# Forgetting bias in the scores' accumulation: one table of cumulative sums for block 1's attention

## The chip, the cores and the metric

The kernel runs on one core of a Trainium2 chip. The metric is the device time of one execution in microseconds (us). The engines are PE (TensorE, matmuls; PEld is its weight load), DVE (VectorE), ACT (ScalarE), POOL and SP; SP issues the weight transfers. Lines of the kernel are written L1204.

## What is computed

Two transformer blocks run one after the other on 256 tokens of width 1024. Block 1 has a causal pooling branch and a "forgetting" attention of 16 heads of 64, block 2 has two other attentions, and each block ends with a retrieval layer over 16384 experts. Only the forgetting attention is touched by the change:

```python
F = jnp.transpose(jnp.cumsum(log_f.astype(jnp.float32), axis=1), (0, 2, 1))
...
    s = jnp.einsum('bqhd,bkhd->bhqk', q[:, q0:L], k[:, :L]) * scale
    s = s + F[:, :, q0:L, None] - F[:, :, None, :L]
    s = jnp.where(kpos[None, :] <= qpos[:, None], s, NEG_INF)
    p = jax.nn.softmax(s, axis=-1).astype(v.dtype)
```

`log_f` is one number for each token and head. A score gets the cumulative sum at its query's position and loses the one at its key's. The first of the two is the same along a row of scores, and a softmax over the row does not depend on it.

## The kernel before

Both blocks are written as one program in which each engine's order is the order of the code. A `Stream` loads the weights in units of 1 MB through SP into three raw buffers (`raw`), ACT makes the high half (`hi`, L138) and DVE the low half (`lo`, L141), and PE multiplies in three passes (hi by hi, lo by hi, hi by lo). In the mixer of block 1 the function `mm_et` (L442) makes a quarter of q, k, the pooling input or the gates from two half units of 24 matmuls each, and `mm_te` (L484) makes v. The units' order is `names1`: v0 q0 k0 v1 q1 k1 p0 p1 v2 q2 k2 v3 q3 k3 a0 to a3 b0 to b3. Results go to two PSUM tiles (`mm`) in turn, and ACT takes them out: kT and qT at L1320, the gates `sga` at L1330 with a sigmoid, for which ACT loads another table than for the exponentials.

Attention is woven in between these groups of 24. `Weave.tick` is called after each group and runs at most four tasks. One of them is `attn_all`, which keeps up to four pairs of heads alive and at each tick moves at most two of them one step on; `attn(hp)` is a generator whose `yield`s are the ends of its steps. There are eight pairs. A pair's steps before the change are:

1. The bias: PE makes for each head of the pair the sum of `lf` up to each key, spread over all 128 rows, by multiplying with the constant `ncum` (-8 on and above the diagonal; 8 is what the scale of the scores takes back): L1204 adds up the first 128 tokens for all 256 keys, L1206 the second 128 tokens for the keys 128 to 255. DVE adds the query's own sum `f8` and the causal mask to it and writes `fm` (L1210, 256 columns, and L1212, 128 columns).
2. The scores: PE multiplies q and k, 64 rows for a head, the first head of the pair on rows 0 to 63 and the second on rows 64 to 127 (L1222 with 256 columns for the second query block, L1223 with 128 for the first). DVE adds `fm` and takes the maximum (L1226, L1228), and ACT makes the exponentials (L1232, L1234).
3. DVE multiplies with the reciprocal of the sums.
4. PE transposes the weights (L1246 to L1248), DVE and ACT copy them to `pt`.
5. PE multiplies with v (L1258, L1260), 64 result rows for a head, and ACT copies the result to `oT`.

All of the attention's operands are fp32, and each of its matmuls is executed as two instructions; the weight matmuls are one instruction each. `forget` makes `lf` ahead of all this from the forget logits (L1176, L1183), and at its end `f8` with three small matmuls (L1194 to L1196).

Of the kernel before, what the change touches and what calls it, by code (L numbers as in the profile page):

```python
# [9 lines left out]
F32 = mybir.dt.float32  # L10
# [4 lines left out]
OP = mybir.AluOpType  # L15
AX = mybir.AxisListType

S = 256
# [4 lines left out]
LOWEST = -3.0e38  # L23
# [11 lines left out]
WHOLE = (18,)  # L35
Y1, Y2, Y3, Y4 = 1, 2, 3, 3
WIDE1 = 1
# [159 lines left out]
def kernel(  # L197
# [29 lines left out]
    V, A, PE, GP = nc.vector, nc.scalar, nc.tensor, nc.gpsimd  # L227
# [9 lines left out]

    # ---------------------------------------------------------- constants
    xpool = [ctx.enter_context(ExitStack())]
# [19 lines left out]
    ident = keep.tile([128, 128], F32, name="ident")  # L259
# [11 lines left out]

    # ---------------------------------------------------------- modulation
    modc = [keep.tile([128, 6, 8], F32, name=f"modc{b}") for b in range(2)]
# [83 lines left out]
    order = [(b, j) for b in range(2) for j in (1, 0, 2, 3, 4, 5)]  # L357
# [9 lines left out]

    # ---------------------------------------------------------- unit order
    last_v, first_v, xnext = [], [], []
# [55 lines left out]

    # ---------------------------------------------------------- helpers
    small = ctx.enter_context(tc.tile_pool(name="small", bufs=2))
# [184 lines left out]

    # ---------------------------------------------------------- PEER
    def peer(b, plan, keys_d, gelu, xs):
# [472 lines left out]

    # ---------------------------------------------------------- block 1 mixer
    with ExitStack() as mx:
        pa = mx.enter_context(tc.tile_pool(name="mix1", bufs=1))  # L1090
# [3 lines left out]
        cs = {k: ct[:, a - 128:b - 128] for k, (a, b) in off.items() if a >= 128}  # L1094
# [5 lines left out]
        def at():  # L1100
            return ps.tile([128, 512], F32, name="at", tag="at")
# [7 lines left out]
        qT = pa.tile([128, 8, S], F32, name="qT")  # L1109
        kT = pa.tile([128, 8, S], F32, name="kT")  # L1110
# [12 lines left out]
        r = rsqrt_seed([ms[:, tt:tt + 1] for tt in range(2)], base)  # L1123
# [42 lines left out]
        lf = pa.tile([128, 2, 16], F32, name="lf")  # L1166
        f8 = pa.tile([128, 2, 16], F32, name="f8")

        def forget():
            split_small(wf, wfh, wfl)  # L1170
            yield 1
            p = at()
# [8 lines left out]
            p = at()  # L1181
# [11 lines left out]
            p = at()  # L1193
            PE.matmul(p[:, 0:16], lhsT=cs["ncum"][:, 0:128], rhs=lf[:, 0, :], start=True, stop=True)  # L1194
            PE.matmul(p[:, 16:32], lhsT=cs["ncum"][:, 128:256], rhs=lf[:, 0, :], start=True, stop=False)
            PE.matmul(p[:, 16:32], lhsT=cs["ncum"][:, 0:128], rhs=lf[:, 1, :], start=False, stop=True)  # L1196
            V.tensor_scalar(f8.rearrange("p a b -> p (a b)"), p[:, 0:32], -1.0, None, op0=OP.mult)

        def attn(hp):
            fm = pa.tile([128, 2, 384], F32, name="fm", tag="fm", bufs=1)  # L1200
            p = at().rearrange("p (a k) -> p a k", a=2)
            for j in range(2):
                h = 2 * hp + j
                PE.matmul(p[:, j, :], lhsT=lf[:, 0, h:h + 1].to_broadcast([128, 128]),  # L1204
                          rhs=cs["ncum"], start=True, stop=False)
                PE.matmul(p[:, j, 128:256], lhsT=lf[:, 1, h:h + 1].to_broadcast([128, 128]),  # L1206
                          rhs=cs["ncum"][:, 0:128], start=False, stop=True)
            for j in range(2):
                h = 2 * hp + j
                V.scalar_tensor_tensor(fm[:, j, 0:256], p[:, j, :], f8[:, 1, h:h + 1],  # L1210
                                       cs["cmask"], op0=OP.add, op1=OP.add)
                V.scalar_tensor_tensor(fm[:, j, 256:384], p[:, j, 0:128], f8[:, 0, h:h + 1],  # L1212
                                       cs["cmask"][:, 128:256], op0=OP.add, op1=OP.add)
            yield Y1
            pm = pa.tile([128, 2, 384], F32, name="pm", tag="pm", bufs=LIVE)
# [3 lines left out]
            for j in range(2):  # L1219
                r = slice(64 * j, 64 * j + 64)  # L1220
                p = at()
                PE.matmul(p[:, 0:256], lhsT=qT[r, hp, 128:256], rhs=kT[r, hp, :], start=True, stop=True)  # L1222
                PE.matmul(p[:, 256:384], lhsT=qT[r, hp, 0:128], rhs=kT[r, hp, 0:128], start=True, stop=True)  # L1223
                tiles.append(p)
            for j in range(2):
                V.tensor_tensor_reduce(pm[:, j, 0:256], tiles[j][:, 0:256], fm[:, j, 0:256], 1.0, LOWEST,  # L1226
                                       OP.add, OP.max, m[:, 2 * j:2 * j + 1])
                V.tensor_tensor_reduce(pm[:, j, 256:384], tiles[j][:, 256:384], fm[:, j, 256:384], 1.0, LOWEST,  # L1228
                                       OP.add, OP.max, m[:, 2 * j + 1:2 * j + 2])
            V.tensor_scalar(m, m, -0.125, None, op0=OP.mult)  # L1230
# [117 lines left out]

    # ---------------------------------------------------------- block 2 mixer
    with ExitStack() as mx:  # L1350
# [310 lines left out]
```

## Time and profile before

| | |
|---|---|
| median of 3 runs | 2098.63 us |
| lowest and highest run | 2094.62, 2100.15 us |
| span of the profiled execution | 2093.1 us |
| median of the runs less that span | 5.5 us |
| PE busy | 2050.3 us (98%) |
| DVE busy | 1603.1 us (77%) |
| ACT busy | 986.8 us (47%) |

The profiled execution has no time of its own beside its span; the span runs from its first to its last instruction. "Busy" counts a matmul from its start to its modelled end, and these overlap, so how long a matmul holds PE is read from the starts of the ones that follow each other. In the rows a matmul's shape in the array stands as rows*columns: 128*128 is the whole array, 64*128 half of its rows, 128*64 half of its columns, 16*128 sixteen rows.

### The profile page before, as it was taken

How to read it: one execution, taken by the hardware profiler on the slowest of the kernel's cores; microseconds unless marked ns; L12 is line 12 of the kernel's file. 1: busy time of each engine (PE TensorE's matmuls, PEld its weight loads, DVE VectorE, ACT ScalarE, POOL GpSimd, SP SyncE). 2: the span in 40 equal slices, each digit the busy share in tenths (PEclk: the TensorE clock that was granted, in tenths of full speed). 3: DMA queues.
4: the chain of work that ended last, by engine and by line, in shares of the span. 5: the costliest groups of instructions: out<-in, count | busy, mean ns of one | idle time of the engine just before them, and what ended most of it. 6: DMA issues, size and time to landing. Idle time of an engine off the chain costs nothing.

```text
span 2093.1 us, 37810 instructions
## 1 busy us (share of the span) xinstructions
PE 2050.3 (98%) x15694; PEld 1885.9 (90%) x15694; DVE 1603.1 (77%) x2937; ACT 986.8 (47%) x1307; POOL 5.6 (0%) x15
## 2 busy tenths in 40 slices
PE   5999999999999999999999999999999999999998
PEld 4999999999999877888899999999999998778886
DVE  6787698868876799777668557988588766996556
ACT  4446455544344434444554455555443444344444
POOL 0000000000000000000000000000000000000000
PEclk8999999999999999999989999999999999999999
DMA  8555545554447644588445345555544475445563
GB/s 346 210 218 202 181 164 198 183 184 171 165 168 266 239 161 163 208 333 306 184 174 201 132 141 182 180 183 184 199 163 162 165 259 200 156 168 181 190 222 121
DMA packets 57211, 408.83 MB, mean 195 GB/s; under 512 B 6352, under 2 KB 6736, under 8 KB 8016
## 3 DMA queue, kind: packets, MB, share of 16 engines
q1 hardware_dynamic: 55424, 397.76, 53.4%
q0 software_dynamic: 1296, 8.52, 1.2%
q8 instruction: 123, 2.02, 0.4%
q14 instruction: 48, 0.39, 0.1%
q10 hardware_dynamic: 320, 0.14, 0.0%
HBM read 403.26 MB, written 3.15 MB: 194 GB/s over the span
## 4 chain that ended last, share of the span: by engine, by line
PE 91%; DVE 4%; ACT 2%; DMA 2%; issue 1%; SPq 0%; ACTq 0%; DVEq 0%
PE mm L442 46%; PE acc L897 31%; PE mm L484 2%; PE mm L580 2%; PE g L834 2%; PE g L835 1%; DVE lo L141 1%; PE acc L984 1%; DVE macc L334 1%; DMA raw<-in_w_in_dram 1%; ACT hi L138 1%; PE g L766 1%; PE acc L880 1%; PE mm L458 1%; PE mm L290 0%
## 5 line engine op out<-in xcount | busy, mean ns | idle before, releaser
L141 DVE TENSOR_TENSOR lo<-raw,hi 128x1024 fp32r<-128x1024 f32 x632 | 766.2, 1221 | 366.2 <-ACT hi L138 365.0
L138 ACT ACTIVATE hi<-raw 128x1024 fp32r<-128x1024 f32 x632 | 663.5, 1055 | 490.8 <-PE acc L897 226.5
L442 PE MATMUL mm<-hhi,hi 128*128 128x256 f32 x2848 | 399.8, 282 | 1.9 <-ACT sga L1330 1.6
L442 PE MATMUL mm<-hlo,hi 128*128 128x256 f32 x2848 | 392.9, 280 | 0.0
L442 PE MATMUL mm<-hhi,lo 128*128 128x256 f32 x2848 | 392.7, 280 | 0.0
L442 PEld LDWEIGHTS mm<-hhi,hi 128*128 128x128 f32 x2848 | 359.8, 188 | 6.2 <-ACT sga L1330 1.8
L442 PEld LDWEIGHTS mm<-hhi,lo 128*128 128x128 f32 x2848 | 358.0, 188 | 0.0
L442 PEld LDWEIGHTS mm<-hlo,hi 128*128 128x128 f32 x2848 | 357.9, 188 | 0.0
L897 PE MATMUL acc<-hi,whi 128*128 128x512 f32 x976 | 307.1, 396 | 0.7 <-ACT whi L545 0.7
L897 PE MATMUL acc<-lo,whi 128*128 128x512 f32 x976 | 301.9, 391 | 0.0
L897 PE MATMUL acc<-hi,wlo 128*128 128x512 f32 x976 | 300.6, 389 | 0.0
L897 PEld LDWEIGHTS acc<-hi,wlo 128*128 128x128 f32 x976 | 183.2, 188 | 39.6
L897 PEld LDWEIGHTS acc<-lo,whi 128*128 128x128 f32 x976 | 183.2, 188 | 39.1
L897 PEld LDWEIGHTS acc<-hi,whi 128*128 128x128 f32 x976 | 177.2, 188 | 33.5 <-ACT whi L545 1.6
L636 ACT ACTIVATE ringa<-mm 128x512 f32<-128x512 f32 x80 | 47.9, 599 | 111.6 <-PE mm L442 111.6
L827 DVE TENSOR_TENSOR gg<-b,gT 128x512 f16<-128x512 f16 x256 | 96.2, 417 | 0.0
L824 DVE TENSOR_TENSOR b<-iota,idx2T 128x1024 f16<-128x1024 f16 x128 | 87.5, 683 | 0.0
L545 ACT ACTIVATE whi<-ringa 128x512 fp32r<-128x512 f32 x78 | 48.8, 628 | 77.3 <-PE acc L897 77.3
L834 PEld LDWEIGHTS <-b 128*128 128x128 f16 x1024 | 63.4, 98 | 20.2 <-issue 8.3
L834 PE MATMUL g<-gg,b 128*128 128x64 f16 x1024 | 78.2, 194 | 0.1
L835 PE MATMUL g<-gg,b 128*128 128x64 f16 x1024 | 77.0, 193 | 0.0
L636 ACT ACTIVATE ringb<-mm 128x512 f32<-128x512 f32 x48 | 28.7, 599 | 93.8 <-PE mm L442 93.8
(359 smaller groups left out, 1837.5 us busy)
## 6 DMA issues: line engine op xcount, KB each, us to landing
raw<-in_peer_u_dram SPq DMA_DIRECT2D x128, 1024.0 KB, 4.9
raw<-in_peer_v_dram SPq DMA_DIRECT2D x118, 1024.0 KB, 4.9
raw<-in_w_in_dram SPq DMA_DIRECT2D x45, 1024.0 KB, 5.0
raw<-in_w_mod_dram SPq DMA_DIRECT2D x20, 1024.0 KB, 5.0
raw<-in_w_ada_dram SPq DMA_DIRECT2D x20, 1024.0 KB, 5.4
ringa<-in_peer_v_dram SPq DMA_DIRECT2D x10, 1024.0 KB, 5.6
raw<-in_w_out_dram SPq DMA_DIRECT2D x8, 1024.0 KB, 4.9
raw<-in_w_query_dram SPq DMA_DIRECT2D x8, 1024.0 KB, 4.9
```

The source lines that it names most:

```text
L138: self.nc.scalar.activation(hi, src, AF.Copy)
L141: self.nc.vector.tensor_sub(lo, src, hi.bitcast(F32))
L442: PE.matmul(ps[:, j, :], lhsT=w[:, k, :], rhs=h[:, k, :], start=n == 0 and k == 0, stop=n == 2 and k == 7)
L484: PE.matmul(ps[:, tt, :], lhsT=h[:, 4 * p + k, tt * 128:(tt + 1) * 128], rhs=w[:, k, :], start=p == 0 and tt == 0 and i == 0, stop=p == 1 ...
L545: A.activation(hi, src, AF.Copy)
L580: PE.matmul(acc[q][:, tt, :], lhsT=h[:, 4 * p + k, tt * 128:(tt + 1) * 128], rhs=w[:, k, :], start=p == 0 and tt == 0 and i == 0, stop=p = ...
L636: state["evac"] = lambda: A.activation(slots(p), ps, gelu)
L824: V.tensor_tensor(pairs(b2), lanes(0, 128), each(idx2T[:, c], 128), op=OP.is_equal)
L827: V.tensor_tensor(pairs(gg[:, :, i, :]), pairs(b1), each(gT[:, c, i, :], 64), op=OP.mult)
L834: PE.matmul(ps[:, t, :], lhsT=b2[:, t, :], rhs=gg[:, t, 0, :], start=True, stop=False)
L835: PE.matmul(ps[:, t, :], lhsT=b2[:, t, :], rhs=gg[:, t, 1, :], start=False, stop=True)
L897: PE.matmul(acc[tt][dh], lhsT=w[:, j, tt * 128:(tt + 1) * 128], rhs=v[:, dh * 512:(dh + 1) * 512], start=p == 0 and j == 0 and n == 0, sto ...
```

## The change

`forget` ends with another table: `fk`, 16 rows (one for each head) by 256 tokens, with -8 times the cumulative sum. Two matmuls make it (256 and 128 columns, 16 result rows), and DVE copies it to SBUF. `attn` has no step for the bias any more: for each head a matmul with a column of the identity, spread to 128 columns, picks the head's row of `fk` and writes it on all 128 rows of the scores' PSUM tile, and the matmul of q and k adds to it. DVE adds the constant mask in place of `fm`. `fm`, `f8` and their DVE passes are gone, and with them the query's own sum.

```diff
-        f8 = pa.tile([128, 2, 16], F32, name="f8")
+        fk = pa.tile([16, S], F32, name="fk")
...
-            PE.matmul(p[:, 0:16], lhsT=cs["ncum"][:, 0:128], rhs=lf[:, 0, :], start=True, stop=True)
-            PE.matmul(p[:, 16:32], lhsT=cs["ncum"][:, 128:256], rhs=lf[:, 0, :], start=True, stop=False)
-            PE.matmul(p[:, 16:32], lhsT=cs["ncum"][:, 0:128], rhs=lf[:, 1, :], start=False, stop=True)
-            V.tensor_scalar(f8.rearrange("p a b -> p (a b)"), p[:, 0:32], -1.0, None, op0=OP.mult)
+            PE.matmul(p[0:16, 0:256], lhsT=lf[:, 0, :], rhs=cs["ncum"], start=True, stop=False)
+            PE.matmul(p[0:16, 128:256], lhsT=lf[:, 1, :], rhs=cs["ncum"][:, 0:128], start=False, stop=True)
+            V.tensor_copy(fk, p[0:16, 0:256])
 
         def attn(hp):
-            fm = pa.tile([128, 2, 384], F32, name="fm", tag="fm", bufs=1)
-            p = at().rearrange("p (a k) -> p a k", a=2)
-            for j in range(2):
-                h = 2 * hp + j
-                PE.matmul(p[:, j, :], lhsT=lf[:, 0, h:h + 1].to_broadcast([128, 128]),
-                          rhs=cs["ncum"], start=True, stop=False)
-                PE.matmul(p[:, j, 128:256], lhsT=lf[:, 1, h:h + 1].to_broadcast([128, 128]),
-                          rhs=cs["ncum"][:, 0:128], start=False, stop=True)
-            for j in range(2):
-                h = 2 * hp + j
-                V.scalar_tensor_tensor(fm[:, j, 0:256], p[:, j, :], f8[:, 1, h:h + 1],
-                                       cs["cmask"], op0=OP.add, op1=OP.add)
-                V.scalar_tensor_tensor(fm[:, j, 256:384], p[:, j, 0:128], f8[:, 0, h:h + 1],
-                                       cs["cmask"][:, 128:256], op0=OP.add, op1=OP.add)
-            yield Y1
...
             for j in range(2):
                 r = slice(64 * j, 64 * j + 64)
                 p = at()
-                PE.matmul(p[:, 0:256], lhsT=qT[r, hp, 128:256], rhs=kT[r, hp, :], start=True, stop=True)
-                PE.matmul(p[:, 256:384], lhsT=qT[r, hp, 0:128], rhs=kT[r, hp, 0:128], start=True, stop=True)
+                row = ident[0:16, 2 * hp + j:2 * hp + j + 1].to_broadcast([16, 128])
+                PE.matmul(p[:, 0:256], lhsT=row, rhs=fk, start=True, stop=False)
+                PE.matmul(p[:, 0:256], lhsT=qT[r, hp, 128:256], rhs=kT[r, hp, :], start=False, stop=True)
+                PE.matmul(p[:, 256:384], lhsT=row, rhs=fk[:, 0:128], start=True, stop=False)
+                PE.matmul(p[:, 256:384], lhsT=qT[r, hp, 0:128], rhs=kT[r, hp, 0:128], start=False, stop=True)
                 tiles.append(p)
             for j in range(2):
-                V.tensor_tensor_reduce(pm[:, j, 0:256], tiles[j][:, 0:256], fm[:, j, 0:256], 1.0, LOWEST,
+                V.tensor_tensor_reduce(pm[:, j, 0:256], tiles[j][:, 0:256], cs["cmask"], 1.0, LOWEST,
                                        OP.add, OP.max, m[:, 2 * j:2 * j + 1])
```

The line numbers move: in the changed kernel the bias matmuls are L1207 and L1209, the scores L1208 and L1210, the maximum L1213 and L1215, the exponentials L1219 and L1221, the product with v L1245 and L1247, the gate's evacuation L1317.

PE's order at the first pair of heads, where the first four matmuls of the bias stood before and all eight of the pair stand now:

```order
-L1204 MATMUL at<-cst_108,lf 128x256
-L1206 MATMUL at<-cst_108,lf 128x128
-L1204 MATMUL at<-cst_108,lf 128x256
-L1206 MATMUL at<-cst_108,lf 128x128
+L1207 MATMUL at<-fk,ident 128x256
+L1208 MATMUL at<-kT,qT 128x256
+L1209 MATMUL at<-fk,ident 128x128
+L1210 MATMUL at<-kT,qT 128x128
+L1207 MATMUL at<-fk,ident 128x256
+L1208 MATMUL at<-kT,qT 128x256
+L1209 MATMUL at<-fk,ident 128x128
+L1210 MATMUL at<-kT,qT 128x128
```

The scores stood a group of 24 weight matmuls later, four in a row; now they stand a step earlier and take turns with the bias, and the second head's bias comes between the two heads' scores.

PE's order before at the last pair of heads, whose scores (L1222, L1223) stand right behind another pair's product with v (L1258, L1260); L1300 is a product of the pooling branch:

```order
252 L1258 MATMUL at<-pt,vv 64x256
253 L1260 MATMUL at<-pt,vv 64x128
254 L1258 MATMUL at<-pt,vv 64x256
255 L1260 MATMUL at<-pt,vv 64x128
256 L1222 MATMUL at<-kT,qT 128x256
257 L1223 MATMUL at<-kT,qT 128x128
258 L1222 MATMUL at<-kT,qT 128x256
259 L1223 MATMUL at<-kT,qT 128x128
260 L1300 MATMUL at<-pl,wp 128x256 x2
```

PE's order now at the last pair of heads, from its second head on:

```order
237 L1207 MATMUL at<-fk,ident 128x256
238 L1208 MATMUL at<-kT,qT 128x256
239 L1209 MATMUL at<-fk,ident 128x128
240 L1210 MATMUL at<-kT,qT 128x128
241 L442 MATMUL mm<-hhi,hi 128x256 x8
242 L442 MATMUL mm<-hhi,lo 128x256 x8
243 L442 MATMUL mm<-hlo,hi 128x256 x8
244 L1245 MATMUL at<-pt,vv 64x256
```

A pair's scores now end before a group of weight matmuls and have the product with v behind that group; at three of the eight pairs they followed directly on such a product before, and now at none.

ACT's order around the first gate before (L1330), where the last pair's exponentials (L1232, L1234) come behind two gates:

```order
94 L1330 ACT_TABLE_LOAD
95 L1330 ACTIVATE sga<-mm 128x512
96 L138 ACTIVATE hi<-raw 128x1024 x2
97 L1262 ACTIVATE oT<-at 128x256
98 L1330 ACTIVATE sga<-mm 128x512
99 L138 ACTIVATE hi<-raw 128x1024
100 L1262 ACTIVATE oT<-at 128x256
101 L1232 ACT_TABLE_LOAD
102 L1232 ACTIVATE pm,al<-pm,am 128x256
103 L1234 ACTIVATE pm,al<-pm,am 128x128
```

and now, where the last pair's exponentials (L1219, L1221) stand ahead of the first gate (L1317):

```order
94 L138 ACTIVATE hi<-raw 128x1024
95 L1219 ACTIVATE pm,al<-pm,am 128x256
96 L1221 ACTIVATE pm,al<-pm,am 128x128
97 L1219 ACTIVATE pm,al<-pm,am 128x256
98 L1221 ACTIVATE pm,al<-pm,am 128x128
99 L1317 ACT_TABLE_LOAD
100 L1317 ACTIVATE sga<-mm 128x512
101 L138 ACTIVATE hi<-raw 128x1024
102 L1249 ACTIVATE oT<-at 128x256
```

The last pair moved from behind the gates to ahead of them, and one table load to the exponentials' table and one back are gone.

## Rows read from the trace of the kernel before

**Rows 1.** The page's first part: busy time, share, instructions of each engine.

```profile
span 2093.1 us, 37810 instructions
PE 2050.3 (98%) x15694; PEld 1885.9 (90%) x15694; DVE 1603.1 (77%) x2937; ACT 986.8 (47%) x1307; POOL 5.6 (0%) x15
```

**Rows 2.** Busy time in stretches of 20 us; columns in the first line.

```profile
core 0: us, PE busy (x) PEld busy (x) DVE busy (x) ACT busy (x) POOL busy (x), PEclk, DMA share, GB/s
...
20.00:40.00 20.00, 11.24 (x61) 11.07 (x62) 18.60 (x31) 8.63 (x16) 0.00 (x0) 0.57 0.77 297
...
140.00:160.00 20.00, 19.72 (x160) 18.58 (x158) 15.13 (x33) 9.08 (x18) 0.00 (x0) 1.00 0.54 195
160.00:180.00 20.00, 18.72 (x152) 17.90 (x153) 16.34 (x38) 14.89 (x25) 0.00 (x0) 1.00 0.61 213
...
220.00:240.00 20.00, 18.02 (x132) 17.73 (x131) 14.88 (x38) 10.51 (x25) 0.00 (x0) 0.83 0.30 106
```

**Rows 3.** What PE waited for, 40 to 240 us: total, times, longest.

```profile
PE mm L442 <- ACT sga L1330: 1.6, 1, 1.6
PE at L516 <- DVE modc L300: 1.2, 1, 1.2
```

**Rows 4.** Groups by line, 56 to 176 us: busy us, mean ns, idle before.

```profile
L1210 DVE SCALAR_TENSOR_TENSOR fm<-at,f,cst 128x256 f32<-128x256 f32 x16 | 7.6, 475 | 1.3 <-PE at L1206 1.3
...
L1212 DVE SCALAR_TENSOR_TENSOR fm<-at,f,cst 128x128 f32<-128x128 f32 x16 | 5.5, 341 | 0.0
```

**Rows 5.** PE's timeline at the first pair: start, us, instructions merged.

```profile
63.66 0.64 PE L484 MATMUL mm<-lo,hhi 128*128 128x256 f32 x4
64.14 0.63 PE L484 MATMUL mm<-hi,hlo 128*128 128x256 f32 x4
64.69 0.71 PE L1222 MATMUL at<-kT,qT 64*128 64x256 f32 x4
65.23 0.40 PE L1223 MATMUL at<-kT,qT 64*128 64x128 f32 x4
65.55 0.70 PE L1204 MATMUL at<-cst,lf 128*128 128x256 f32 x2
66.09 0.38 PE L1206 MATMUL at<-cst,lf 128*128 128x128 f32 x2
66.31 0.60 PE L1204 MATMUL at<-cst,lf 128*128 128x256 f32 x2
66.74 0.38 PE L1206 MATMUL at<-cst,lf 128*128 128x128 f32 x2
66.88 1.18 PE L442 MATMUL mm<-hhi,hi 128*128 128x256 f32 x8
```

**Rows 6.** PE's timeline at the last pair, scores behind a product with v.

```profile
164.27 0.66 PE L1258 MATMUL at<-pt,vv 128*64 128x256 f32 x4
164.76 0.40 PE L1260 MATMUL at<-pt,vv 128*64 128x128 f32 x4
165.08 0.71 PE L1222 MATMUL at<-kT,qT 64*128 64x256 f32 x4
165.62 0.40 PE L1223 MATMUL at<-kT,qT 64*128 64x128 f32 x4
```

**Rows 7.** PE's timeline in `forget`: the 16-row transposes, and f8's matmuls.

```profile
47.17 1.09 PE L442 MATMUL mm<-hlo,hi 128*128 128x256 f32 x8
48.20 0.29 PE L1183 MATMUL at<-ident,fT 16*128 16x16 f32 x2
...
54.13 0.29 PE L1194 MATMUL at<-lf,cst 128*128 128x16 f32 x2
...
54.71 0.72 PE L442 MATMUL mm<-hhi,hi 128*128 128x256 f32 x4
```

**Rows 8.** Timeline of ACT, DVE and PE before the first gate's evacuation.

```profile
153.33 1.06 ACT L138 ACTIVATE hi<-raw 128x1024 fp32r<-128x1024 f32 x1 [6.85 <-DMA raw<-in_w_in_dram]
...
156.03 0.41 DVE L1226 CUSTOM_DVE_ANT_0 pm<-at,fm 128x256 f32<-128x256 f32 x1
...
160.63 0.60 ACT L1330 ACTIVATE sga<-mm 128x512 f32<-128x512 f32 x1
...
161.28 1.20 PE L442 MATMUL mm<-hhi,hi 128*128 128x256 f32 x8 [1.56 <-ACT sga L1330]
```

More of the change, by code (lines that the diff above doesn't have):

```diff
@@ L35 @@
 WHOLE = (18,)
-Y1, Y2, Y3, Y4 = 1, 2, 3, 3
+Y2, Y3, Y4 = 2, 3, 3
 WIDE1 = 1
@@ L1221, in attn @@
                 p = at()
-                PE.matmul(p[:, 0:256], lhsT=qT[r, hp, 128:256], rhs=kT[r, hp, :], start=True, stop=True)
-                PE.matmul(p[:, 256:384], lhsT=qT[r, hp, 0:128], rhs=kT[r, hp, 0:128], start=True, stop=True)
+                row = ident[0:16, 2 * hp + j:2 * hp + j + 1].to_broadcast([16, 128])
[3 more added lines that the diff above has]
+                PE.matmul(p[:, 256:384], lhsT=qT[r, hp, 0:128], rhs=kT[r, hp, 0:128], start=False, stop=True)
                 tiles.append(p)
             for j in range(2):
-                V.tensor_tensor_reduce(pm[:, j, 0:256], tiles[j][:, 0:256], fm[:, j, 0:256], 1.0, LOWEST,
+                V.tensor_tensor_reduce(pm[:, j, 0:256], tiles[j][:, 0:256], cs["cmask"], 1.0, LOWEST,
                                        OP.add, OP.max, m[:, 2 * j:2 * j + 1])
-                V.tensor_tensor_reduce(pm[:, j, 256:384], tiles[j][:, 256:384], fm[:, j, 256:384], 1.0, LOWEST,
-                                       OP.add, OP.max, m[:, 2 * j + 1:2 * j + 2])
+                V.tensor_tensor_reduce(pm[:, j, 256:384], tiles[j][:, 256:384], cs["cmask"][:, 128:256], 1.0,
+                                       LOWEST, OP.add, OP.max, m[:, 2 * j + 1:2 * j + 2])
             V.tensor_scalar(m, m, -0.125, None, op0=OP.mult)
```

## The prediction

> **What bounds the kernel now.** I read the first part of the page, then the stretches of 20 us, and last the list of what TensorE (PE) waited for. In the first the reader is to see that PE is busy for 2050.3 of 2093.1 us [rows 1]. The change touches only block 1's mixer, whose scores lie between 64 and 166 us [rows 5, 6]; there the stretches show a granted clock of 1.00 and PE busy for 20 of 20 us, but for 19.72 from 140 and 18.72 from 160 on [rows 2]. In the whole stretch from 40 to 240 us the longest wait of PE is 1.6 us, once, for ScalarE's (ACT's) evacuation of the gate's matmul, L1330 [rows 3]. So this stage is as long as the matmuls that stand in it, and the answer to "what does the change do to the time" is the answer to "what does it do to PE's queue". A saving on VectorE (DVE) has nothing on PE's side to release.
>
> **DVE's part, worth nothing.** Sixteen passes of 475 ns (L1210) and sixteen of 341 ns (L1212) go [rows 4]: 16 x 0.816 = 13.1 us of DVE work. No wait of PE in this stage goes back to them; DVE has 15.13 to 16.34 us of work in 20 [rows 2], and PE is the cover of all of it. The masked maximum (old L1226 and L1228) stays, with the mask in place of fm. One table copy (fk) comes for one small pass (f8). Value: 0.
>
> **PE's part: columns.** The lengths are read from the starts in the timeline. In a steady row of fp32 matmuls the one of 256 columns (L1204, the second one) takes 66.74 - 66.31 = 0.43 us, and the one of 128 (L1206) 66.31 - 66.09 = 0.22 [rows 5]. A pair of heads has two of each for the bias: 1.30 us. Its scores have as many columns, but the two heads use different halves of the rows (64*128), and they run at the same time: from 64.69 to 65.23 all four instructions of L1222 start, both heads' 256 columns, and from 65.23 to 65.55 all of L1223 [rows 5]. So scores need 0.43 + 0.22 = 0.65 of columns, once for both heads. In the changed order each head is bias 256, scores 256, bias 128, scores 128, and each scores matmul adds to what the bias matmul before it wrote, while between the two heads' scores stand the second head's bias matmuls. I take it that nothing runs beside another any more: 4 x 0.65 = 2.60 us of columns per pair. Columns before: 8 x (1.30 + 0.65) = 15.6; after: 8 x 2.60 = 20.8; **+5.2 us**.
>
> **PE's part: changes of the array's shape.** The same rows show what it costs to go from 128 rows to 64 and back. L484 starts four matmuls each 0.48 us (63.66, 64.14), so the next is due at 64.62; the scores start at 64.69: +0.07. Their 256 columns take 0.54, not 0.43: +0.11, the first weights are not loaded ahead. Their 128 columns take 0.32, not 0.22: +0.10 until the next shape can start. The first L1204 then takes 65.55 to 66.09 = 0.54, again +0.11 [rows 5]. Into the shape 0.18, out of it 0.21; I take **0.20 us for each change**. At 164.76 the step from 128*64 (L1260) to 64*128 (L1222) shows +0.10 and +0.11 [rows 6], so it's the change that costs, not the 128 rows. The new bias matmuls have 16 rows. The trace has one such place: L1183 is due at 47.17 + 0.96 = 48.13 and starts at 48.20, +0.07, as the scores do [rows 7]. No row shows 16 rows against 64, which is what the changed kernel does all the time. I bound it from below by nothing (both start at row 0, and the array might treat them as one shape) and from above by 0.21, and take 0.20, since each of the three pairs of shapes in the trace paid on entry.
>
> The count: before, a pair's scores are one stay in the 64-row shape, in and out, 16 changes for eight pairs; three stays follow directly on a 128*64 matmul (old L1260, as in [rows 6] at 165.08) and share that change: 13. After, a pair is eight matmuls that alternate 16 and 64 rows, with 128-row matmuls around all of them: nine changes, 72 for eight pairs, and the new order has none of them beside the 128*64 matmuls. 72 - 13 = 59 changes x 0.20 = **+11.8 us**. The Trainium skill, "TensorEngine Tiling (Array Packing)", Key Properties, speaks against this change: "Changing tiling mode (not just tile) drains the TensorE", and it lists 64x128 and 32x128 as different modes. It gives no time; by it the sum would be this one, with the 59 changes at the measured 0.20.
>
> **The table.** Three small matmuls go (54.13 to 54.71, 0.58 us [rows 7]); one of 256 and one of 128 columns with 16 result columns come, another shape: 0.65 + 2 x 0.20 = 1.05. **+0.5 us**. Behind it stand 48 weight matmuls before the first bias matmul, 48 x 0.12 = 5.8 us, which hide its copy.
>
> **The one wait.** At 161.28 PE had stood for 1.56 us, because sga (160.63) is the end of a chain that began late: ACT waited until 153.33 for a weight transfer, DVE's masked maximum came behind that at 156.03, and from there it takes 161.23 - 156.03 = 5.2 us through the exponentials and a table load [rows 8]. After the change two pairs' exponentials stand ahead of sga, but the first pair's are ready a matmul group earlier. From the last scores to the matmul that needs sga's buffer PE still has two groups of 24 weight matmuls (5.8 us), two 128*64 groups (165.08 - 164.27 = 0.8 each, [rows 6]) and a pool product, about 8 us against the chain's 5.2; and PE is longer at each pair, while transfers take what they took. I take the wait as gone: **-1.6 us**, with 0 as the other end. Two table loads (ACT) go as well; nothing but sga waits for them. What is late next is PE itself. Weight transfers, which made ACT wait 6.85 us there, get more time, not less.
>
> **Sum.** +5.2 + 11.8 + 0.5 - 1.6 = +15.9 us. The profiled span goes from 2093.1 to 2109.0; the median of the runs lies 5.5 us above that span, so 2098.63 + 15.9 = **2114.5 us** (+0.76%). Nothing later gives it back: PE is the bound of the stages behind it too [rows 1]. What a measurement of this kernel can tell from no change is about 0.3%, 6.3 us.
>
> **Rivals.**
> 1. *Changes between 16 and 64 rows are free* (not slower). Then only entries and exits pay, 16 in place of 13: +0.6; 5.2 + 0.6 + 0.5 - 1.6 = +4.7, 2103.3, within 0.3%. For it: both shapes begin at row 0, and no row shows the pair. Against it: 128*64 to 64*128 also share a corner, and paid in full [rows 6]. It decides at 0.03 us for each of the 56 inner changes (4.7 + 56 x 0.03 = 6.4): only a price near zero brings it there.
> 2. *The second head's bias runs beside the scores.* The second head's scores use rows 64 to 127 and could run beside bias matmuls of rows 0 to 15, as the two heads' scores do now. Then the chain through the low rows is 2 x 0.65 for the first head plus 0.65 for the second head's bias, 1.95 a pair, as many columns as before: +0.6 + 0.5 - 1.6, about 2098. Against it: they add into the same PSUM tile in a fixed order. The Trainium skill, "TensorE: Matmul & The Clock Gate", the table "Why this matters for your kernels", says of small contractions that tiles in distinct row groups run concurrent; the 64-row scores agree (four starts of L1222 in one 0.54 us). By that rule the time would be this rival's.
> 3. *The clock falls.* With the array waiting between short matmuls of few rows, the granted clock could go from 2.4 to 1.2 GHz, as it does for part of 20 to 40 us, a mean of 0.57, and of 220 to 240, 0.83; in both PE stood still for a while before [rows 2]. If each of the eight places cost as much as the half-clock part of that last stretch (0.17 x 20 = 3.4 us lost), it would be +27 more: 2142. Against it: the 1.56 us of standing at 161 left 160 to 180 at 1.00.
> 4. *Faster.* DVE, 13.1 us lighter, lets the weight halves be ready earlier. All that PE could win is its 1.6 us of waiting in this stage; over 6.3 us of gain has no place in the rows.
>
> **Chances.** The forecast (each change pays) 0.76, with a range of its own of 2111 (every change at the 0.18 of an entry: +14.7) to 2119 (0.21, and the wait stays: +18.1), each widened by two us for the scatter of the runs, 2094.62 to 2100.15 before; rival 1 0.13, rival 2 0.05, rival 3 0.04, rival 4 0.02. For 8 in 10 the range reaches down to the upper edge of rival 1: 2104 to 2121. Slower by over 0.3%: forecast, rival 3 and a dear form of rival 1, 0.82; within: 0.15; faster: 0.03.
>
> **What would show it.** In the profile after: the bias and scores matmuls of a pair should take about 4.3 us from the first to the next weight matmul (0.63 for each 256 with its change, 0.42 for each 128); no two heads' matmuls at the same start; PE busy at 100% from 160 to 180, with no row for sga among PE's waits; a clock of 1.00; DVE's busy time 13 us lower. It is wrong if scores follow the bias after 0.43 and not 0.54 (rival 1), if L1208 of the second head starts before its bias ended (rival 2), or if PE gets new waits for fk, kT or the PSUM tiles.

## The result, and the profile after

The changed kernel takes 2128.34 us (median of 4 runs, 2126.33 to 2132.4) against 2096.62 us of the kernel before (2093.8 to 2100.15): a ratio of 1.0151, 95% interval 1.0135 to 1.0168. It is slower, as forecast, but by 31.7 us and not by 15.9. The forecast of 2114.5 us and its range, which ended at 2121.0, are both too low.

The page's first part answers [rows 1]:

```profile
span 2124.6 us, 37754 instructions
...
PE 2083.0 (98%) x15692; PEld 1904.6 (90%) x15692; DVE 1595.8 (75%) x2905; ACT 985.1 (46%) x1305; POOL 5.5 (0%) x15
```

DVE has 32 instructions less and 7.3 us less to do (the removed passes were 13.1; many of its other groups became a little longer, L845 for one 489 ns in place of 481), PE's busy time grew by 32.7 us, and the span by 31.5. Next the list of what PE waited for, 40 to 270 us (total, times, longest), which answers [rows 3]:

```profile
PE at L516 <- DVE modc L300: 1.2, 1, 1.2
PE mm L458 <- ACT hhi L537: 0.8, 1, 0.8
PE at L1176 <- ACT wfh L545: 0.6, 1, 0.6
```

The wait for `sga` is gone, and no wait for `fk`, `kT` or a PSUM tile took its place. The 31.5 us were lost while PE worked. The L516 row marks a place for measuring: it is the first wait of PE behind block 1's mixer. In PE's timeline it stands in the kernel before and in the changed one at:

```profile
231.66 0.40 PE L516 MATMUL at<-ident,rstd 128*128 128x128 f32 x2 [1.18 <-DVE modc L300]
```

```profile
257.81 0.66 PE L516 MATMUL at<-ident,rstd 128*128 128x128 f32 x2 [1.18 <-DVE modc L300]
```

257.81 - 231.66 = 26.15: of the 31.5 us, 26.2 are lost by the end of the mixer, and 5.3 in the 1867 us behind it. PE's timeline at the first pair (start, us, instructions merged) answers [rows 5]:

```profile
60.36 0.64 PE L484 MATMUL mm<-hi,hlo 128*128 128x256 f32 x4
60.93 0.69 PE L1207 MATMUL at<-fk,ident 16*128 16x256 f32 x2
61.56 0.70 PE L1208 MATMUL at<-kT,qT 64*128 64x256 f32 x2
62.18 0.48 PE L1209 MATMUL at<-fk,ident 16*128 16x128 f32 x2
62.59 0.49 PE L1210 MATMUL at<-kT,qT 64*128 64x128 f32 x2
63.01 0.69 PE L1207 MATMUL at<-fk,ident 16*128 16x256 f32 x2
...
65.09 0.74 PE L484 MATMUL mm<-hi,hhi 128*128 128x256 f32 x4
```

This is the pair that the prediction drew: 0.62 to 0.63 us for each block of 256 columns, 0.41 to 0.42 for each of 128, nothing beside anything else, 65.09 - 60.93 = 4.16 us. With the entry (60.93, due at 60.36 + 0.48 = 60.84) and the 0.11 of the exit it is 4.36 us; the prediction's 4 x 0.65 + 9 x 0.20 is 4.40.

What it had not drawn is in the stretches. In the kernel before, PEclk is 1.00 from 60 to 200 us; in the changed one (columns as in [rows 2]):

```profile
60.00:80.00 20.00, 20.00 (x118) 16.11 (x117) 10.86 (x30) 7.44 (x21) 0.00 (x0) 0.91 0.50 170
...
140.00:160.00 20.00, 20.00 (x107) 17.53 (x107) 10.44 (x28) 8.59 (x22) 0.00 (x0) 0.71 0.32 108
...
60.00:200.00 140.00, 140.00 (x930) 120.51 (x929) 86.41 (x184) 56.06 (x120) 0.00 (x0) 0.91 0.49 175
```

PE is busy for 140.00 of 140 us, and the granted clock is 0.91. It fell from 2.4 to 1.2 GHz at five of the eight pairs, each time within or right behind the pair's matmuls, and the weight matmuls behind ran at the lower clock before it rose again. Such a place in PE's timeline:

```profile
136.96 0.69 PE L1207 MATMUL at<-fk,ident 16*128 16x256 f32 x2
137.58 1.05 PE L1208 MATMUL at<-kT,qT 64*128 64x256 f32 x2
138.57 0.79 PE L1209 MATMUL at<-fk,ident 16*128 16x128 f32 x2
139.28 0.79 PE L1210 MATMUL at<-kT,qT 64*128 64x128 f32 x2
140.01 1.22 PE L484 MATMUL mm<-hi,hhi 128*128 128x256 f32 x4
```

L1208 takes 0.99 us to the next start where it took 0.62 at the first pair, and the row of four L484 matmuls behind the pair lasts 1.22 us where it lasted 0.74. If half clock were half speed, the time lost would be the missing share times the stretch: (1 - 0.91) x 140 = 12.6 us. It is a little less, since four weight matmuls that start 0.48 us apart at full clock [rows 5] start 0.86 apart at half clock (66.97 and 67.83 in the rows of the 16-row kernel below): 0.38 of each 0.86 us is lost, 0.44 and not 0.50. By this estimate 12.6 becomes about 11. So the 26.2 us of the mixer are about 15 of work at full clock, against 15.9 forecast, and about 11 of half clock. The fall of the clock is rival 3, which had a chance of 0.04. Its reason, "the array waiting", isn't what the rows show: PE has no wait there. The experiments ask what it is.

### The profile page after: what moved, and what is told of

It reads as the page before. It is cut to its first block, busy times and chain, and to the rows that moved or that the text cites. A ratio compares the mean times of both kernels' runs of the same rounds, so it can differ in the third digit from the quotient of the medians.

```text
span 2124.6 us, 37754 instructions
## 1 busy us (share of the span) xinstructions
PE 2083.0 (98%) x15692; PEld 1904.6 (90%) x15692; DVE 1595.8 (75%) x2905; ACT 985.1 (46%) x1305; POOL 5.5 (0%) x15
## 4 chain that ended last, share of the span: by engine, by line
PE 93%; DVE 3%; ACT 1%; DMA 1%; issue 0%; SPq 0%; ACTq 0%; DVEq 0%
PE mm L442 47%; PE acc L897 30%; PE mm L484 2%; PE mm L580 2%; PE g L834 1%; PE g L835 1%; PE acc L984 1%; DVE lo L141 1%; DVE macc L334 1%; ACT hi L138 1%; PE mm L290 1%; PE g L766 1%; PE acc L880 1%; DMA raw<-in_peer_u_dram 1%; PE mm L458 1%; PE at L1208 1%
```

## Experiments

All are changes to the changed kernel; their diffs are against it. Three explanations of the 16 us by which the forecast fell short are to be told apart. **Few rows:** matmuls of 16 rows, many in a row, let the clock fall though PE is busy. **Drains:** the nine changes of shape per pair, at each of which the array stands for a moment, let it fall. **Not the clock:** the missing time is in the matmuls themselves, wherever they stand, and the low clock only goes along with it.

### The two heads a group apart

```diff
                 tiles.append(p)
+                if j == 0:
+                    yield 1
```

> The changed kernel, but the second head's bias and scores are a step of their own, one group of 24 weight matmuls later. Every matmul stays; a pair's eight are two fours with five changes of shape each, 80 in all, not 72. Theory A (the clock falls because eight short matmuls that wait for the array's shape follow each other for 4.2 us): no place is long enough, the granted clock stays 1.00 in the mixer, and the time is the sum of the prediction with 8 more changes: 2096.6 + 5.2 + 13.4 + 0.5 - 1.6 = 2114. Theory B (the 16 rows themselves, or any alternating, bring the clock down): the falls stay, and the time stays at 2126 to 2130. Theory C (the rest of the loss is not the clock's): the clock may go up and the time not come down.

Measured: 2117.44 us (2116.74 to 2118.72), ratio 1.0097 (1.0080 to 1.0114). This is between the 2114 expected if no place is long enough for a fall and the 2126 to 2130 if the falls stay. The matmuls are the same and only stand apart, with three changes of shape more and not fewer, and 10.9 us of the 31.7 are gone. In the mixer it is 257.81 - 252.40 = 5.4 us by the L516 row; the other half lies behind it and in the scatter of the runs. The granted clock:

```profile
60.00:200.00 140.00, 140.00 (x973) 120.39 (x972) 87.83 (x187) 61.55 (x125) 0.00 (x0) 0.96 0.52 188
```

By the shares it lost (1 - 0.96) x 140 = 5.6 us, or about 5 at the price above, where the changed kernel lost about 11: that is the mixer's gain. The clock fell at two places. The sixteen heads make fourteen such places, since at two of them the last head of one pair and the first of another happened to meet; the clock fell at these two and at none of the twelve where a head stood alone. PE's timeline at the first of the two:

```profile
67.71 0.49 PE L1210 MATMUL at<-kT,qT 64*128 64x128 f32 x2
68.12 0.77 PE L1207 MATMUL at<-fk,ident 16*128 16x256 f32 x2
68.82 1.22 PE L1208 MATMUL at<-kT,qT 64*128 64x256 f32 x2
...
71.41 2.07 PE L442 MATMUL mm<-hhi,hi 128*128 128x256 f32 x8
```

So the falls go with what stands in a row. The third explanation, that the clock only goes along, falls, since the same work costs less when it is spread. Few rows and drains remain, for both were spread alike.

### The bias of both heads first, then the scores

The four bias matmuls of a pair stand together and its scores behind them, so that a pair has three changes of shape instead of nine, and the two heads' scores are neighbours again.

```diff
-                PE.matmul(p[:, 0:256], lhsT=row, rhs=fk, start=True, stop=False)
-                PE.matmul(p[:, 0:256], lhsT=qT[r, hp, 128:256], rhs=kT[r, hp, :], start=False, stop=True)
-                PE.matmul(p[:, 256:384], lhsT=row, rhs=fk[:, 0:128], start=True, stop=False)
...
+                PE.matmul(p[:, 0:256], lhsT=row, rhs=fk, start=True, stop=False, skip_group_check=True)
+                PE.matmul(p[:, 256:384], lhsT=row, rhs=fk[:, 0:128], start=False, stop=False,
+                          skip_group_check=True)
                 tiles.append(p)
             for j in range(2):
+                r = slice(64 * j, 64 * j + 64)
...
+                PE.matmul(p[:, 0:256], lhsT=qT[r, hp, 128:256], rhs=kT[r, hp, :], start=False, stop=False,
+                          skip_group_check=True)
```

> The changed kernel with the four bias matmuls of a pair first and then its four scores matmuls: three changes of shape a pair (24), and nothing stands between the two heads' scores. If a change costs 0.20 us and scores run side by side whenever nothing of another shape stands between them: columns as before (8 x 1.95), 24 in place of 13 changes: +2.2 + 0.5 - 1.6 = +1.1, 2097.7, clock 1.00 in the mixer. If the 16 rows of the bias alone bring the clock down (theory B), some falls stay and it is 2105 or more. DVE's 13 us are gone here too; if they were worth anything, this run would be below the kernel before by more than the one wait of 1.6.

Measured: 2098.36 us (2098.06 to 2100.29), ratio 1.0010 (1.0001 to 1.0020). PE's timeline at the first pair:

```profile
60.81 0.69 PE L1206 MATMUL at<-fk,ident 16*128 16x256 f32 x2
...
62.31 0.71 PE L1213 MATMUL at<-kT,qT 64*128 64x256 f32 x4
62.85 0.39 PE L1215 MATMUL at<-kT,qT 64*128 64x128 f32 x4
63.17 0.50 PE L484 MATMUL mm<-hi,hhi 128*128 128x256 f32 x2
```

A pair takes 63.17 - 60.81 = 2.36 us, and four instructions of each scores line are merged, as in [rows 5]: the heads run beside each other. The clock is 1.00 over the whole mixer. This kernel has all of the change but its order, the saved DVE passes included, and it's level with the kernel before: the loss hangs on the order, and no gain from the DVE passes shows.

### The same order, the bias from 128 rows

The table is widened with 112 rows of zeros. Order, columns and values are those of the changed kernel, and a bias matmul has the weight matmuls' shape.

```diff
-        fk = pa.tile([16, S], F32, name="fk")
+        fk = pa.tile([128, S], F32, name="fk")
+        lw = pa.tile([128, 2, 128], F32, name="lw")
+        V.memset(lw, 0.0)
...
-                row = ident[0:16, 2 * hp + j:2 * hp + j + 1].to_broadcast([16, 128])
+                row = ident[:, 2 * hp + j:2 * hp + j + 1].to_broadcast([128, 128])
```

> The changed kernel with the table on all 128 rows, 112 of them zero, so that the bias matmuls use the whole array; order and number of changes of shape (72) as in the changed kernel. Theory A (waiting brings the clock down, whatever the rows): falls as in the changed kernel, 2122 to 2130. Theory B (few rows bring it down): no falls, 2096.6 + 5.2 + 11.8 + 0.1 - 1.6 = 2112. It also measures 128 against 64 rows: per pair 4.2 us as with 16 rows, if a change costs the same between all shapes.

Measured: 2110.81 us (2110.24 to 2112.58), ratio 1.0068 (1.0051 to 1.0085). PE's timeline of the pair, and the stretch:

```profile
61.31 0.59 PE L1210 MATMUL at<-fk,ident 128*128 128x256 f32 x2
61.83 0.70 PE L1211 MATMUL at<-kT,qT 64*128 64x256 f32 x2
...
65.38 0.74 PE L484 MATMUL mm<-hi,hhi 128*128 128x256 f32 x4
```

```profile
60.00:200.00 140.00, 140.00 (x1025) 121.85 (x1025) 92.64 (x192) 60.48 (x127) 0.00 (x0) 1.00 0.55 196
```

A pair takes 65.38 - 61.31 = 4.07 us: 128 against 64 rows costs what 16 against 64 does, less the one entry that a 128-row bias behind a weight matmul doesn't pay (eight changes a pair, not nine). The clock stays at 1.00, with nearly all of the changes of shape still there. So the drains fall as the cause, and this is the time that the prediction's own terms give: with 64 changes in place of 72 their sum is 5.2 + 51 x 0.20 + 0.5 - 1.6 = +14.3, and the medians differ by 2110.81 - 2096.7 = 14.1. Between this kernel and the changed one lie 17.5 us, of which the eight changes are 1.6.

### Few rows by themselves, longer

To separate the rows from the changes of shape altogether, the kernel with the bias of both heads first is taken with each bias matmul made three times, each time starting the sum anew: 3.9 us of 16-row matmuls in a row, with no change of shape among them. The other kernel does the same from 128 rows.

```diff
+                for again in range(3):
+                    PE.matmul(p[:, 0:256], lhsT=row, rhs=fk, start=True, stop=False, skip_group_check=True)
+                    PE.matmul(p[:, 256:384], lhsT=row, rhs=fk[:, 0:128], start=False, stop=False,
+                              skip_group_check=True)
```

> e2_bias_first with the four 16-row bias matmuls of a pair made three times over (the last one counts): 3.9 us of 16-row work in a row, without waits between, then the scores; changes of shape stay at 24. If few rows and waiting are both needed for the clock to fall, it stays 1.00 in the mixer: e2_bias_first + 8 x 2.6 = 2098.4 + 20.8 = 2119.2. If few rows alone do it (theory B), there are falls at several of the eight places and it is 2123 to 2133, with the half clock in the rows.

> e7_16_rows_long with its table on all 128 rows, 112 of them zero: the same 24 long bias matmuls in a row for each pair, the same lengths, on the whole array; 16 changes of shape, not 24. If few rows bring the clock down, it stays 1.00 in the mixer here and the time is e7's without its falls and with 8 changes fewer: 2096.9 + 20.8 + 0.6 + 0.9 - 1.6 = 2117.6. If long stretches of these matmuls do it whatever the rows, it is 2135 to 2143 as e7 was.

Measured: 2141.12 us (2138.3 to 2143.41), ratio 1.0210 (1.0194 to 1.0225), from 16 rows, and 2118.22 us (2116.96 to 2120.19), ratio 1.0101 (1.0084 to 1.0118), from 128. The stretches, first of 16 rows, then of 128:

```profile
60.00:200.00 140.00, 140.00 (x925) 129.11 (x925) 72.82 (x161) 47.98 (x109) 0.00 (x0) 0.84 0.42 151
```

```profile
60.00:200.00 140.00, 140.00 (x1102) 132.41 (x1101) 87.69 (x187) 58.70 (x125) 0.00 (x0) 1.00 0.52 186
```

From 128 rows 2117.6 was expected, and from 16 rows 2123 to 2133, with falls at several pairs. But the clock fell at each of the eight. Of the 22.9 us between the two kernels (1 - 0.84) x 140 = 22.4 us, or about 20 at the price above, are the clock's, and 1.6 the eight changes of shape that the 16-row kernel has more. PE's timeline of the 16-row kernel at the first pair, from the last bias matmul on:

```profile
64.93 0.38 PE L1208 MATMUL at<-fk,ident 16*128 16x128 f32 x2
65.24 0.71 PE L1214 MATMUL at<-kT,qT 64*128 64x256 f32 x4
...
66.10 1.07 PE L484 MATMUL mm<-hi,hhi 128*128 128x256 f32 x4
66.97 1.05 PE L484 MATMUL mm<-lo,hhi 128*128 128x256 f32 x4
67.83 1.05 PE L484 MATMUL mm<-hi,hlo 128*128 128x256 f32 x4
```

At this pair the bias matmuls themselves run at full speed, and the weight matmuls behind them pay, 67.83 - 66.97 = 0.86 us for four in place of 0.48. At five of the eight pairs the fall comes while the bias matmuls still run; at the second pair the L1207 that starts at 73.61 takes 0.85 us to the next start, not 0.43. Few rows alone do it, without a wait and without changes of shape among them. The 128-row kernel differs in its zeros and in eight changes of shape fewer, and the kernel with the bias first has those changes at a clock of 1.00. So it's the rows that a matmul spans that count here, not the values in them.

### The bias on the head's own 64 rows

If shapes must agree, the nearest is that of the scores. The table lies on rows 0 to 15 and again on rows 64 to 79, with zeros between, and each head takes its bias from its own half.

```diff
+            V.tensor_copy(lw[:, :, 0:16], lf)
+            V.tensor_copy(lw[:, :, 64:80], lf)
...
-                PE.matmul(p[:, 0:256], lhsT=row, rhs=fk, start=True, stop=False)
+                row = ident[r, 65 * j + 2 * hp:65 * j + 2 * hp + 1].to_broadcast([64, 128])
+                PE.matmul(p[:, 0:256], lhsT=row, rhs=fk[r, :], start=True, stop=False)
```

> The changed kernel with the table twice, at rows 0 and 64, zero between, and each bias matmul on the 64 rows that its head's scores use: bias and scores of a head have one shape and one place, so two changes a pair, and the two heads can run side by side. If they do: 1.30 + 2 x 0.20 = 1.70 us a pair against 8 pairs = 18.2 before: -4.6, with -1.6 for the wait and +0.1 for the table: 2090.5, faster than the kernel before by 0.3%. If adding to a bias keeps the heads from running side by side: 2.6 + 0.4 = 3.0 a pair, 2101. The clock stays 1.00 in the mixer in both.

Measured: 2100.6 us (2098.11 to 2103.15), ratio 1.0015 (1.0005 to 1.0024). PE's timeline at the first pair:

```profile
61.29 0.69 PE L1211 MATMUL at<-fk,ident 64*128 64x256 f32 x2
61.82 0.59 PE L1212 MATMUL at<-kT,qT 64*128 64x256 f32 x2
62.26 0.27 PE L1213 MATMUL at<-fk,ident 64*128 64x128 f32 x1
62.26 0.48 PE L1211 MATMUL at<-fk,ident 64*128 64x256 f32 x1
...
63.76 0.74 PE L484 MATMUL mm<-hi,hhi 128*128 128x256 f32 x4
```

Bias and scores follow each other without a change (62.26 - 61.82 = 0.44), but the second head starts only at 62.26, when the first has its two 256-column matmuls behind it: a pair takes 2.47 us, and no more than the middle of it is shared. That lies between the two prices expected, 1.70 and 3.0. The next kernel keeps the table and deals the matmuls out in turn: bias 256 of both heads, scores 256 of both, bias 128 of both, scores 128 of both.

```diff
+            tiles = [at(), at()]
+            for j, r in enumerate(rows):
+                PE.matmul(tiles[j][:, 0:256], lhsT=one[j], rhs=fk[r, :], start=True, stop=False)
+            for j, r in enumerate(rows):
+                PE.matmul(tiles[j][:, 0:256], lhsT=qT[r, hp, 128:256], rhs=kT[r, hp, :], start=False, stop=True)
...
```

> The run with the bias on 64 rows (e4_64_rows), with the two heads in turn: bias of both, scores of both over 256 columns, then the same over 128. In e4_64_rows the second head started only when the first had four matmuls done, so 2.15 us a pair went where 1.30 is needed. If neighbours in the queue run side by side whenever their rows differ: 1.30 + 2 x 0.20 = 1.70 us a pair, -4.6 in all, -1.6 for the wait, +0.8 for the table: 2091.3. If a matmul that adds to a bias has to wait for it with a drain: 2.15 a pair as in e4_64_rows, -1.0 - 1.6 + 0.8, 2095. The clock stays 1.00 in the mixer.

Measured: 2091.53 us (2088.97 to 2092.33), ratio 0.9970 (0.9959 to 0.9982).

```profile
60.66 0.70 PE L1211 MATMUL at<-fk,ident 64*128 64x256 f32 x4
61.20 0.60 PE L1213 MATMUL at<-kT,qT 64*128 64x256 f32 x4
61.63 0.39 PE L1215 MATMUL at<-fk,ident 64*128 64x128 f32 x4
61.85 0.39 PE L1217 MATMUL at<-kT,qT 64*128 64x128 f32 x4
62.17 0.74 PE L484 MATMUL mm<-hi,hhi 128*128 128x256 f32 x4
```

All four lines run for both heads at once, a pair takes 62.17 - 60.66 = 1.51 us in place of 4.16 (and of 2.47 in the kernel above, which the expectation puts at 2.15), and the idea of the change now beats the kernel before by 0.3%. The order is worth the 0.96 us per pair between these two kernels. The Trainium skill, "TensorEngine Tiling (Array Packing)", Key Properties, says that different tiles can load and multiply in parallel; these rows agree, for accumulating matmuls too. Here it took neighbours of one shape on different rows, each head with a PSUM tile of its own, dealt out in turn.

### The bias in two halves and one pass

Each number of the table is split into a high and a low half, on rows 32 apart, and the ones that pick it stand in both rows, so that the bias is one instruction and not two.

```diff
-        fk = pa.tile([16, S], F32, name="fk")
+        fk = pa.tile([128, S], F32R, name="fk")
...
+            for i in (32, 96):
+                V.tensor_sub(fk[i:i + 32, :], p[i:i + 32, 0:256], fk[i:i + 32, :].bitcast(F32))
```

> e5_64_in_turn with the table split into a high and a low half (rows 0 and 32 of each 64), so that one bias matmul in the weights' format, a single instruction, brings in both: 0.12 us for 256 columns and 0.06 for 128 in place of 0.43 and 0.22. A pair: 0.18 + 0.65 + 0.40 = 1.23 us against 18.2 for eight pairs before: -8.4, -1.6, +0.9 for the table: 2087.6. If the 128-column one takes as long as fp32 does, 0.2 more a pair: 2089. If the step between the two formats costs a change, 2 more a pair, +3.2: 2091.

Measured: 2089.27 us (2088.11 to 2092.64), ratio 0.9965 (0.9953 to 0.9977). In PE's timeline at the first pair:

```profile
60.31 0.38 PE L1218 MATMUL at<-fk,selr 64*128 64x256 f32 x2
60.53 0.59 PE L1220 MATMUL at<-kT,qT 64*128 64x256 f32 x4
60.77 0.41 PE L1222 MATMUL at<-fk,selr 64*128 64x128 f32 x2
61.02 0.44 PE L1224 MATMUL at<-kT,qT 64*128 64x128 f32 x4
61.38 0.74 PE L484 MATMUL mm<-hi,hhi 128*128 128x256 f32 x4
```

A pair takes 1.07 us in place of 1.51. The 256-column bias takes 0.22 to the next start, where the two-instruction form took 61.20 - 60.66 = 0.54. The 128-column one can't be read from its own start, since at 60.77 the scores' second instructions, begun at 60.74, still run; from scores to scores it is 61.02 - 60.53 = 0.49 where it was 61.85 - 61.20 = 0.65. This is the fastest kernel of the study. Its interval overlaps with that of the one before it, so only its gain over the two kernels of the change is measured, not the last 2 us.

### The changed kernel once more

One more profile of it, to see whether the places of the fall are fixed.

> The changed kernel once more, for a second profile of it. If the falls of the clock hang on the places alone, the same five stretches are at half clock; if they hang on when a place comes, other ones of the eight are, with about the same sum, and the time is 2126 to 2133 again.

Measured: 2128.41 us, one execution. The stretch, the second head's first scores of the first pair, and the first wait behind the mixer:

```profile
60.00:200.00 140.00, 140.00 (x890) 119.27 (x890) 82.29 (x179) 54.18 (x118) 0.00 (x0) 0.88 0.48 167
...
63.95 1.13 PE L1208 MATMUL at<-kT,qT 64*128 64x256 f32 x2
...
262.73 0.66 PE L516 MATMUL at<-ident,rstd 128*128 128x128 f32 x2 [1.18 <-DVE modc L300]
```

The clock fell at six pairs: at the five of the first time (the second, third, fifth, sixth and seventh pair) and also at the first, whose L1208 lasts 1.13 us here and 0.70 there. By the shares it lost (1 - 0.88) x 140 = 16.8 us, or about 15 at the price above. The L516 row comes 262.73 - 231.66 = 31.1 us later than in the kernel before, so about 16 of these are work at full clock. So over two executions five places agree: the fourth and the eighth pair kept the clock both times, the first only once. Why stays open.

## Why the prediction was wrong

**Right: what bounds, and DVE's part at nothing.** PE bounds the stage, and the second experiment has the DVE saving without the new order and gains nothing. Of the signs, DVE's busy time fell by 7.3 us and not by 13.

**Right: columns and changes of shape.** 4.36 us per pair against 4.40. The one price that no row showed, 16 rows against 64, was bounded by 0 and 0.21 and taken at 0.20: L1208 starts 0.63 us after L1207, and 0.63 - 0.43 = 0.20. (The prediction named this step twice, as 0.63 and, in its last sentence, as 0.54; the first held.) Rival 1 (free changes) falls by this, and so does rival 2 (the second head's bias beside the scores): nothing of a pair runs at the same time. Whether the difference of shapes or the PSUM tile that a head's bias and scores share keeps them apart, no run separates: in the kernel dealt out in turn both heads run at once, with bias and scores adding up, but each head has its own tile. The sentence on draining in the Trainium skill, "TensorEngine Tiling (Array Packing)", Key Properties, held, at that price.

**Right: the table and the wait.** The first bias matmul starts 0.47 us later than the first one before (60.93 and 60.46), 0.09 of it its own entry, against 0.5 forecast for the table, and the `sga` row is gone.

**The sum of these terms** was +15.9. The changed kernel's mixer without its lost clock has about +15 in the first profile and about +16 in the second, and the kernel with 128 rows, at full clock and with eight changes fewer, has the +14.1 in the medians that these terms give.

**Wrong: the dismissal of rival 3.** The step that failed put the clock's loss at nothing in the sum, by the one sentence "Against it: the 1.56 us of standing at 161 left 160 to 180 at 1.00". The runs show about 11 and about 15 us in its place. The sentence tested the wrong condition. Both rows that showed a low clock had PE standing, so the prediction took standing for the cause and asked only whether PE would stand; in the changed order it never does. Standing is no sure sign either: from 20 to 40 us, where PE stands for 8 to 9 us, the clock is 0.57 in the changed kernel's first profile and 1.00 in its second. The rows of before held no stretch in which PE was busy for microseconds with few rows, so they could not speak for or against it, and the 0.04 had no row behind it. The rival's size was off the other way: eight falls at 3.4 us were put at 27, for the clock fell at five or six pairs and not always for that long. With the 11 of the first profile the forecast's +15.9 becomes about +27, where the mixer has +26.2 and the whole kernel +31.7 in the medians.

The Trainium skill, "TensorE: Matmul & The Clock Gate", Part 1, ties the clock to how busy PE has been and names idle gaps as what lowers it. By that rule the changed kernel would keep its clock. The trace differs: PEclk is 0.91 at 140.00 busy us of 140, with no wait between, and the measurement decides.

**A smaller fault:** the median was set 5.5 us above the profiled span. The runs after the change lie 1.7 us above their own spans (2126.33 and 2124.6), so most of these 5.5 us were scatter between runs of the kernel before. With the fourth run its median is 2096.62, and the forecast counted from there is 2112.5.

**Open:** 5.3 of the 31.5 us come behind the mixer, where the two kernels have the same instructions. Half-clock stretches that the kernel before has as well are longer there in the changed one (before, 220 to 240 us at 0.83 [rows 2], 3.4 us lost; after, 240 to 400 at 0.97 with the same place of the program in it, 4.8 lost), but every other kernel has 1.5 to 4.0 us more than the kernel before behind its own L516 row too. In the second profile of the changed kernel it is 2.4 us (2126.6 - 262.73 against 2093.1 - 231.66), so about half of the 5.3 belongs to the one execution. No run separates the rest from the scatter of the runs. Open too is where between 16 and 128 rows the falls end: the two kernels with the bias on 64 rows kept the clock at 1.00, but with 1.51 and 2.47 us at a pair and not 4.16.

## What to carry to other kernels

Before you put a small contraction among large matmuls, write down the shape of each in the array, count the changes of shape in the new order (0.20 us each here), and see which neighbours still share a shape on different rows: zeros up to the neighbour's shape cost no time on PE here (0.43 us for 256 columns on 16, 64 and 128 rows), and dealing two heads out in turn took a pair from 4.16 to 1.51 us. A PE that is busy for 100% isn't a PE at full clock: here four microseconds of matmuls on 16 rows, alone or in turn with 64, brought it down to 1.2 GHz, and the large ones behind took 0.86 us where they take 0.48. Where the trace of before has no row for a rival's condition, rows of another condition say nothing against it.

## What the runs showed of the hardware

- The granted clock fell with PE busy throughout: 0.91 and 0.88 from 60 to 200 us with 16-row matmuls between 64-row ones, 0.84 with 3.9 us of 16-row matmuls in a row at each pair, 1.00 in both cases with the same matmuls on 128 rows, of which 112 held zeros. Twelve single heads (four matmuls, about 2.1 us) left it at 1.00.
- A change between 16 and 64 rows costs what one between 128 and 64 does, 0.20 us, and going from one 64-row matmul to another, from bias to scores, costs nothing (61.63 - 61.20 = 0.43).
- How early a matmul on the other half of the rows starts went with its place in the order: with the second head's first matmul four places behind the first head's it waited for two of these, 0.97 us; with the heads in turn it started with them. Why isn't shown.
